# Conv norm of a hybrid encoder layer: means from split sums as fp32r products, and reciprocals issued block by block

## The chip, the cores and the metric

The kernel runs on one core of a Trainium2 chip. The metric is the device time of one execution in microseconds. A change of about 0.2% (2.9 us here) is what a measurement can tell from no change. The core's engines run side by side, each through its own instructions in its own order: TensorE (PE in the profile; its weight loads are PEld), VectorE (DVE), ScalarE (ACT), GpSimd (POOL) and SyncE (SP), which here issues most transfers.

## The reference

One layer of a streaming encoder: one input projection feeds a convolution branch, an attention branch and two gates. The means and variances of the convolution branch are what is changed.

```python
def _layer_norm(x, g, b):
    xf = x.astype(jnp.float32)
    mu = jnp.mean(xf, axis=-1, keepdims=True)
    var = jnp.mean(jnp.square(xf - mu), axis=-1, keepdims=True)
    y = (xf - mu) * lax.rsqrt(var + LN_EPS) * g.astype(jnp.float32) + b.astype(jnp.float32)
    return y.astype(x.dtype)

def _conv_branch(u_ext, w_dw, b_dw, ln_g, ln_b, w_out):
    y = lax.conv_general_dilated(...)            # depthwise, width 31, over 512 channels
    y = jax.nn.silu(_layer_norm(y + b_dw, ln_g, ln_b))
    return jnp.einsum('btc,cd->btd', y, w_out)

# in the layer
u, q, k, v, logf, g_conv, g_attn = _in_proj(x, w_in, b_f)
y_conv = _conv_branch(...)
o_attn = _fox_prompt(q, k, v, logf)             # softmax attention with forget gates
mix = (g_conv * y_conv + g_attn * (o_attn @ w_attn_out)) @ w_o
x1 = layer_norm(ALPHA * x + mix); x2 = layer_norm(ALPHA * x1 + relu(x1 @ w_up)**2 @ w_down)
```

There are 1056 rows (1024 of a new stream, 32 of a running one), 1024 model channels, 512 conv channels, 8 heads of 64.

## The kernel before

**Precision.** Channels lie on the 128 partitions, rows along the free axis. A product of full precision is made of three fp32r products of high and low parts: `hi` is a copy in fp32r (made by ScalarE), `lo` is the value less `hi` (made by VectorE). The weights (`whi`, `wlo`, from `raw`) are split in this way in pieces of 512 columns, ahead of their use.

**Stages.** In the first one (pool `conv`, pool `a`) TensorE makes the projections for the convolution, for v, q and k, and then the first 6 of 16 gate tiles (`gates`). A gate tile is 3 chunks of 352 rows; a chunk is 24 products of 128x352 into one PSUM bank (`ps_g`), which ScalarE copies to `gt` and SyncE writes to memory (`g_s`). In the second stage (pools `b` and `pb`) come attention and, as filling between its products, gates 6 to 15. There the chunks have two PSUM banks (`bbank`: `tag="acc", bufs=2`) and two staging tiles (`GB = 2`).

**The conv branch beside it.** VectorE makes the depthwise convolution and the norm as a generator (`conv`) that is asked for its next piece while TensorE is given projections. The norm works on three blocks of 362 columns (`CC`), each of four tiles `ca`. For each block: the sum of four tiles (`lns_m`), a product with a matrix of 1/512 on TensorE that spreads the mean over all partitions (`ps_mu_c`), subtraction from the four tiles (VectorE), squares (`sq_c`, ScalarE), their sum (`lns_v`), a second such product (`ps_var_c`), a square root (`rstd_c`, ScalarE, which needs a table load before and after it) and its reciprocal (VectorE, in place). Then twelve pieces (block, tile): scale by `rstd_c`, a sigmoid on ScalarE (`csig`), a multiplication, a split into `csh` (ScalarE) and `csl` (VectorE), and four or two writes (`s_s`).

**What sets the order.** The program keeps times of its own for every engine while it writes the instructions (class `Issue`). A generator goes on when what it waits for is due by those times, for a mean 3000 ns after its sum (`MARGIN`). The order in which the instructions are written is the order in which TensorE, VectorE, ScalarE and GpSimd run them; SyncE's is set by a scheduler. When the first stage has no gate left, `I.flush()` writes all that remains of the conv branch, and only then is the second stage written, starting with a table load for the exponential (`tiny`).

Of the kernel before, what the change touches and what calls it, by code (L numbers as in the profile page):

```python
# [9 lines left out]
F32 = mybir.dt.float32  # L10
F32R = mybir.dt.float32r
BF16 = mybir.dt.bfloat16
AF = mybir.ActivationFunctionType
# [4 lines left out]
P = 128  # L18
# [8 lines left out]
C_CONV = 512  # L27
# [12 lines left out]
CC = NC // 3  # L40
# [14 lines left out]
MARGIN = 3000.0  # L55
# [25 lines left out]
class Issue:  # L81
# [116 lines left out]
    def dma(self, out, in_, queue=None):  # L198
        self.run("dma", max(450, Issue.size(out) * out.shape[0] * 4 / 360), [out], [in_])
        out, in_ = (t.bitcast(F32) if t.dtype == F32R else t for t in (out, in_))  # L200
        (queue or self.nc.sync).dma_start(out, in_)

    def mm(self, ps, w, x, start, stop):
        n = self.size(ps)
        self.run("pe", 122 if n == CB else max(107, n / 2.36) if x.dtype != F32 else max(430, n * 1.71), [ps], [w, x])
        self.nc.tensor.matmul(ps, lhsT=w, rhs=x, start=start, stop=stop)  # L206
# [5 lines left out]
    def act(self, out, in_, func, bias=None, **kw):  # L212
        aps = [] if bias is None else [bias]
        self.run("act", self.size(in_) * 0.81 + (62 if self.psum(in_) else 103) + 93 * len(aps),
                 [out] + [v for k, v in kw.items() if k == "accum_out"], [in_] + aps)
        if bias is not None:
            kw["bias"] = bias
        self.nc.scalar.activation(out, in_, func, **kw)  # L218
# [5 lines left out]
    def tt(self, out, a, b, op, eng="dve"):  # L224
        n = self.size(out)
        self.run(eng, n * 1.01 + 80 if eng == "dve" else n * 1.97 + 150, [out], [a, b])
        (self.nc.vector if eng == "dve" else self.nc.gpsimd).tensor_tensor(out, a, b, op)  # L227

    def ts(self, out, a, s1, s2, *ops):
        self.run("dve", self.size(out) * (1.01 if self.psum(a) else 0.51) + 130, [out], [a])  # L230
        self.nc.vector.tensor_scalar(out, a, s1, s2, *ops)

    def stt(self, out, a, s, b, op0, op1):
        self.run("dve", self.size(out) * 1.01 + 140, [out], [a, b])
        self.nc.vector.scalar_tensor_tensor(out, a, s, b, op0, op1)  # L235
# [27 lines left out]
def f32(t):  # L263
    return t.bitcast(F32)
# [3 lines left out]
def hybrid_layer(ctx: ExitStack, tc, io):  # L268
    nc = tc.nc
    I = Issue(nc)  # L270
    dma, mm, act, cp, tt, ts, stt = I.dma, I.mm, I.act, I.cp, I.tt, I.ts, I.stt
    ADD, SUB, MUL, MAX, MIN = ALU.add, ALU.subtract, ALU.mult, ALU.max, ALU.min
# [31 lines left out]
    def par(name, j):  # L304
        return prm[:, PRM[name] + j:PRM[name] + j + 1]
# [186 lines left out]
    with pool("conv") as pv_, pool("a") as pa, pool("pa", space=PSUM) as psa:  # L492
        num = [0]

        def bank(name):
            num[0] += 1
            return psa.tile([P, 512], F32, tag="acc", bufs=8, name=f"ps_{name}_{num[0]}")
# [55 lines left out]
        need_x(4)  # L553
        ones = pa.tile([P, P], F32, name="ones")
        nc.gpsimd.memset(ones, 1.0)
        mean_c = pv_.tile([P, P], F32, name="mean_c")
        nc.gpsimd.memset(mean_c, 1.0 / C_CONV)
        mean_d = const.tile([P, P], F32, name="mean_d")
        nc.gpsimd.memset(mean_d, 1.0 / D)
        zt = pa.tile([P, 9, H], F32, name="zt")  # L560
# [52 lines left out]
        def conv():  # L613
            for j in range(NJ):
                w = [par("w_dw", j * WID + t) for t in range(WID)]
                yield [u[j]]
                ts(ca[j], u[j][:, 0:NC], w[0], par("b_dw", j), MUL, ADD)
                for t in range(1, WID):
                    yield ("dve", 1500)
                    stt(ca[j], u[j][:, t:t + NC], w[t], ca[j], MUL, ADD)  # L620

            blocks = [slice(c * CC, (c + 1) * CC) for c in range(3)]
            tiles = [[ca[j][:, cs] for j in range(NJ)] for cs in blocks]

            def summed(kind, c, src):
                a = pv_.tile([P, CC], F32, tag="lns", bufs=3, name=f"lns_{kind}{c}")
                tt(a, src[0], src[1], ADD)
                for t in src[2:]:
                    tt(a, a, t, ADD)
                return a  # L630

            sums, rstds = [], []
            for c in range(3):
                sums.append(summed("m", c, tiles[c]))
                yield ("dve", 1500)
            for c in range(3):
                yield (MARGIN, [sums[c]])
                mu = bank(f"mu_c{c}")[:, :CC]
                mm(mu, mean_c, sums[c], True, True)
                sq = []  # L640
                for i, t in enumerate(tiles[c]):
                    tt(t, t, mu, SUB)
                    sq.append(pv_.tile([P, CC], F32, tag="lnsq", bufs=4, name=f"sq{i}_c{c}"))
                    act(sq[-1], t, AF.Square)
                sums[c] = summed("v", c, sq)
            for c in range(3):
                yield (MARGIN, [sums[c]])
                var = bank(f"var_c{c}")[:, :CC]
                mm(var, mean_c, sums[c], True, True)
                rstds.append(pv_.tile([P, CC], F32, tag="lnrstd", bufs=3, name=f"rstd_c{c}"))  # L650
                act(rstds[-1], var, AF.Sqrt, bias=eps)
            for r in rstds:
                yield ("dve", 1500)
                I.recip(r, r)
            pieces = [(c, j) for c in range(3) for j in range(NJ)]
            late = last = None
            for piece in pieces + [None, None]:
                yield ("dve", 1500)
                if piece:
                    c, j = piece  # L660
                    y = tiles[c][j]
                    stt(y, y, par("lcg", j), rstds[c], MUL, MUL)
                    sg = pv_.tile([P, CC], F32, tag="csig", bufs=2, name=f"csig{c}_{j}")
                    act(sg, y, AF.Sigmoid, bias=par("lcb", j))
                before, last = last, None
                if late:
                    c, j, z, s = late
                    stt(z, z, par("lcb", j), s, ADD, MUL)
                    hi, lo = (pv_.tile([P, CC], F32R, tag=x, bufs=4, name=f"{x}{c}_{j}") for x in ("csh", "csl"))
                    act(hi, z, AF.Copy)  # L670
                    last = c, j, z, hi, lo
                if before:
                    c, j, z, hi, lo = before
                    tt(lo, z, f32(hi), SUB)
                    for dst, src in ((s_s[0][j], hi), (s_s[1][j], lo)):
                        if c < 2:
                            dma(dst[:, blocks[c]], src)
                        else:
                            e = SEQ - 2 * CC
                            dma(dst[:, 2 * CC:SEQ], src[:, :e])  # L680
                            dma(dst[:, SEQ:T], src[:, CC - DEC:])
                late = (*piece, y, sg) if piece else None
# [47 lines left out]
        for c in range(NCH):  # L730
# [3 lines left out]
            for kind in "ba":  # L734
                glu(kind, 0, c)
                if c == NCH - 1:
                    W.drop()
        I.add(conv(), "conv")
        for j in range(1, NJ):
            for kind in "ba":  # L740
# [11 lines left out]
        for half in range(2):  # L752
            ws = [W.take() for g in range(2)]
            for t in range(9):
# [6 lines left out]
                r = P if t < 8 else DEC  # L761
# [33 lines left out]
        for m in range(4):  # L795
            for name in "qk":
                w = W.take()
                for c in range(NCH):
                    ps = bank(name)[:, :CH]
                    dense(ps, on_x(w, c))  # L800
                    a = pa.tile([P, CH], F32, tag="qk32", bufs=2, name=f"{name}32_{m}_{c}")
# [380 lines left out]
    def cbank(name, tag="acc", bufs=5):  # L1182
        num[0] += 1
        return bank_pool[0].tile([P, 512], F32, tag=tag, bufs=bufs, name=f"ps_{name}_{num[0]}")
# [17 lines left out]
    def tmp(tag, bufs, name):  # L1202
        return ln_pool[0].tile([P, LNW], F32, tag=tag, bufs=bufs, name=name)
# [65 lines left out]
    with pool("ps1", space=PSUM) as bank_pool[0]:  # L1269
# [60 lines left out]
        with pool("l1") as ln_pool[0]:  # L1330
# [60 lines left out]
            for group in GROUPS:  # L1391
                sums = {}
# [51 lines left out]
            sums = combine()  # L1444
            for n, (f, b) in enumerate(order):
# [11 lines left out]
                r = tmp("rp", 5, f"r{f}_{b}")  # L1457
# [343 lines left out]
    for i, cs in enumerate(tail):  # L1801
# [15 lines left out]
        for m in range(KD):  # L1817
            ps = more(m)
            a = acc[m][:, cs]
# [10 lines left out]
    n, tag = cs.stop - cs.start, "n2_last"  # L1830
    tiles = [a[:, cs] for a in acc]
    nth, sq, var, s, held_ps = len(turned), [], None, None, {}
# [24 lines left out]
    mu = cbank("mu_last", "mu", 2)[:, :n]  # L1857
# [122 lines left out]
```

## Time and profile before

| | |
|---|---|
| median of 3 runs | 1444.24 us (1443.33 to 1444.28) |
| the profiled execution | 1444.01 us, its span 1441.4 us, 2.6 us around it |
| TensorE busy | 1425.4 us, 99% of the span |
| VectorE busy | 1119.5 us, 78% |
| ScalarE busy | 683.0 us, 47% |
| granted TensorE clock | 0.998 of full speed |

The stage with the conv norm lies between 263 and 316 us of the span, and the second stage's first gate chunks follow it. A wait of TensorE adds to the time almost one for one; idle time of the others costs nothing by itself.

### The profile page before, as it was taken

What the parts mean: (1) busy time and instruction counts of PE and PEld (TensorE: products, weight loads), DVE (VectorE), ACT (ScalarE), POOL (GpSimd) and SP (SyncE); (2) the same over time, 40 slices, a digit from 0 to 9 for tenths busy, and PEclk for the clock granted to TensorE, in tenths of its full rate; (3) what the DMA queues carried; (4) which work ended last, traced back from release to release, by engine and by line L of the source; (5) the groups of instructions that cost most, each with busy time, mean ns of one, the idle gap of its engine ahead of it and who ended that gap; (6) DMA issues with size and microseconds to landing.
All of it is one profiled execution on the core that took longest, in us unless ns stands there. A gap on an engine that the chain in (4) does not pass through costs nothing.

```text
span 1441.4 us, 27988 instructions
## 1 busy us (share of the span) xinstructions
PE 1425.4 (99%) x10623; PEld 1404.0 (97%) x10623; DVE 1119.5 (78%) x1929; ACT 683.0 (47%) x1446; POOL 124.2 (9%) x183
## 2 busy tenths in 40 slices
PE   9999999999999999999999999999999999999996
PEld 8999999999999999999999999999999999999996
DVE  6998899865666655855797888888976789889668
ACT  5123433465665656543345666676657323321134
POOL 0000000023455533000000000000000000000000
PEclk9999999999999999999999999999999999999999
DMA  7125554287455557425343348766689999884212
GB/s 249 46 61 161 171 172 157 88 273 209 111 152 157 154 153 264 144 83 177 94 135 124 130 151 296 251 239 231 225 287 344 335 317 333 276 321 176 67 45 77
DMA packets 157441, 267.91 MB, mean 186 GB/s; under 512 B 22680, under 2 KB 81272, under 8 KB 157308
## 3 DMA queue, kind: packets, MB, share of 16 engines
q1 hardware_dynamic: 156348, 263.98, 55.4%
q0 software_dynamic: 544, 1.59, 0.5%
q8 instruction: 84, 1.38, 0.4%
q10 hardware_dynamic: 416, 0.56, 0.1%
q14 instruction: 49, 0.40, 0.1%
HBM read 168.29 MB, written 97.74 MB: 185 GB/s over the span
## 4 chain that ended last, share of the span: by engine, by line
PE 97%; DVE 1%; DMA 1%; ACT 0%; issue 0%; SPq 0%; DVEq 0%
PE ps_u L206 18%; PE ps_d L206 17%; PE ps_g L206 13%; PE ps_dn L206 6%; PE ps_o L206 6%; PE ps_up L206 5%; PE ps_v L206 3%; PE ps_yc L206 3%; PE ps_k L206 3%; PE ps_glua L206 3%; PE ps_q L206 3%; PE ps_glub L206 3%; PE ps_yo L206 3%; PE ps_s L206 3%; PE ps_pv L206 2%; PE ps_tr L210 2%
## 5 line engine op out<-in xcount | busy, mean ns | idle before, releaser
L235 DVE SCALAR_TENSOR_TENSOR ca<-u,prm,ca 128x1086 f32<-128x1086 f32 x120 | 161.7, 1347 | 2.4
L206 PE MATMUL ps_g<-xh,whi 128*128 128x352 f32 x384 | 131.7, 343 | 0.0
L218 ACT ACTIVATE swhi<-s 128x512 fp32r<-128x512 f32 x100 | 61.9, 624 | 146.9 <-DVE s L227 134.0
L206 PE MATMUL ps_g<-xh,wlo 128*128 128x352 f32 x384 | 123.7, 322 | 0.0
L206 PE MATMUL ps_g<-xl,whi 128*128 128x352 f32 x384 | 121.5, 322 | 0.0
L206 PE MATMUL ps_u<-tl,swhi 128*128 128x264 f32 x416 | 118.4, 285 | 0.0
L206 PE MATMUL ps_u<-th,swhi 128*128 128x264 f32 x416 | 118.2, 284 | 0.0
L206 PE MATMUL ps_u<-th,swlo 128*128 128x264 f32 x416 | 118.2, 284 | 0.0
L218 ACT ACTIVATE whi<-raw 128x512 fp32r<-128x512 f32 (+1 forms) x120 | 69.6, 624 | 69.6 <-PE ps_glua L206 29.7
L227 DVE TENSOR_TENSOR tl<-ps_tr,th 128x512 fp32r<-128x512 f32 (+2 forms) x96 | 51.4, 552 | 60.2 <-ACT th L218 59.5
L206 PE MATMUL ps_d<-hu_h,swhi 128*128 128x264 f32 x480 | 93.0, 285 | 0.1
L206 PE MATMUL ps_d<-hu_l,swhi 128*128 128x264 f32 x480 | 92.9, 285 | 0.0
L218 ACT ACTIVATE r<-r 128x528 f32<-128x528 f32 (+1 forms) x120 | 73.9, 616 | 37.8 <-DVE r L227 35.5
L227 DVE TENSOR_TENSOR wlo<-raw,whi 128x512 fp32r<-128x512 f32 (+1 forms) x100 | 64.8, 686 | 29.1 <-ACT whi L218 28.9
L227 DVE TENSOR_TENSOR r<-r,ps_u 128x528 f32<-128x528 f32 x91 | 62.6, 699 | 29.6 <-PE ps_u L206 29.6
L206 PEld LDWEIGHTS ps_u<-th,swhi 128*128 128x128 f32 x416 | 78.3, 188 | 0.0
L206 PEld LDWEIGHTS ps_u<-th,swlo 128*128 128x128 f32 x416 | 78.3, 188 | 0.0
L206 PEld LDWEIGHTS ps_u<-tl,swhi 128*128 128x128 f32 x416 | 78.2, 188 | 0.0
L227 POOL TENSOR_TENSOR acc<-acc,lnrest 128x288 f32<-128x288 f32 x4 | 3.0, 787 | 857.6 <-ACT lnrest L218 857.6
L206 PEld LDWEIGHTS ps_d<-hu_h,swhi 128*128 128x128 f32 x480 | 74.6, 189 | 0.3 <-issue 0.2
L206 PEld LDWEIGHTS ps_d<-hu_l,swhi 128*128 128x128 f32 x480 | 74.6, 189 | 0.0
L206 PEld LDWEIGHTS ps_g<-xh,whi 128*128 128x128 f32 x384 | 72.7, 189 | 0.7
(434 smaller groups left out, 4997.8 us busy)
## 6 DMA issues: line engine op xcount, KB each, us to landing
h_s<-sp SPq DMA_DIRECT2D x84, 528.0 KB
raw<-in_w_in_dram SPq DMA_DIRECT2D x63, 256.0 KB
hu_h<-h_s SPq DMA_DIRECT2D x30, 528.0 KB
hu_l<-h_s SPq DMA_DIRECT2D x30, 528.0 KB
sraw<-in_w_up_dram SPq DMA_DIRECT2D x52, 256.0 KB
hu<-h_s SPq DMA_DIRECT2D x24, 528.0 KB
sraw<-in_w_ds_dram SPq DMA_DIRECT2D x48, 256.0 KB
g_s<-gt SPq DMA_DIRECT2D x48, 176.0 KB
```

Of the source, the lines that this page charges most:

```text
L206: self.nc.tensor.matmul(ps, lhsT=w, rhs=x, start=start, stop=stop)
L210: self.nc.tensor.transpose(ps, x, ident)
L218: self.nc.scalar.activation(out, in_, func, **kw)
L227: (self.nc.vector if eng == "dve" else self.nc.gpsimd).tensor_tensor(out, a, b, op)
L235: self.nc.vector.scalar_tensor_tensor(out, a, s, b, op0, op1)
```

## The change

The sum of each block (for the mean and for the variance) is now split: ScalarE makes a high part `csh` in fp32r, VectorE a low part `csl`. The mean is two fp32r products, high and low, into the same bank, in place of one F32 product; the matrix of 1/512 becomes fp32r. The low part of a block is written behind the sum of the next one; the reciprocal of a block behind the square root of the next one. A pause of the generator is gone in front of two reciprocals. Both parts use the tags of the tiles that hold `csh` and `csl` of the result (four buffers each).

```diff
--- before.py
+++ after.py
@@ -553,8 +553,8 @@
         need_x(4)
         ones = pa.tile([P, P], F32, name="ones")
         nc.gpsimd.memset(ones, 1.0)
-        mean_c = pv_.tile([P, P], F32, name="mean_c")
-        nc.gpsimd.memset(mean_c, 1.0 / C_CONV)
+        mean_c = pv_.tile([P, P], F32R, name="mean_c")
+        nc.gpsimd.memset(f32(mean_c), 1.0 / C_CONV)
         mean_d = const.tile([P, P], F32, name="mean_d")
         nc.gpsimd.memset(mean_d, 1.0 / D)
         zt = pa.tile([P, 9, H], F32, name="zt")
@@ -627,31 +627,47 @@
                 tt(a, src[0], src[1], ADD)
                 for t in src[2:]:
                     tt(a, a, t, ADD)
-                return a
+
+                parts = [pv_.tile([P, CC], F32R, tag=x, bufs=4, name=f"{x}_{kind}{c}") for x in ("csh", "csl")]
+                act(parts[0], a, AF.Copy)
+                return a, parts
+
+            def low(a, parts):
+                tt(parts[1], a, f32(parts[0]), SUB)
+                return parts
 
             sums, rstds = [], []
             for c in range(3):
                 sums.append(summed("m", c, tiles[c]))
+                if c:
+                    sums[c - 1] = low(*sums[c - 1])
                 yield ("dve", 1500)
+            sums[2] = low(*sums[2])
             for c in range(3):
-                yield (MARGIN, [sums[c]])
+                yield (MARGIN, sums[c])
                 mu = bank(f"mu_c{c}")[:, :CC]
-                mm(mu, mean_c, sums[c], True, True)
+                for i, a in enumerate(sums[c]):
+                    mm(mu, mean_c, a, i == 0, i == 1)
                 sq = []
                 for i, t in enumerate(tiles[c]):
                     tt(t, t, mu, SUB)
                     sq.append(pv_.tile([P, CC], F32, tag="lnsq", bufs=4, name=f"sq{i}_c{c}"))
                     act(sq[-1], t, AF.Square)
                 sums[c] = summed("v", c, sq)
+                if c:
+                    sums[c - 1] = low(*sums[c - 1])
+            sums[2] = low(*sums[2])
             for c in range(3):
-                yield (MARGIN, [sums[c]])
+                yield (MARGIN, sums[c])
                 var = bank(f"var_c{c}")[:, :CC]
-                mm(var, mean_c, sums[c], True, True)
+                for i, a in enumerate(sums[c]):
+                    mm(var, mean_c, a, i == 0, i == 1)
                 rstds.append(pv_.tile([P, CC], F32, tag="lnrstd", bufs=3, name=f"rstd_c{c}"))
                 act(rstds[-1], var, AF.Sqrt, bias=eps)
-            for r in rstds:
-                yield ("dve", 1500)
-                I.recip(r, r)
+                if c:
+                    I.recip(rstds[c - 1], rstds[c - 1])
+            yield ("dve", 1500)
+            I.recip(rstds[2], rstds[2])
             pieces = [(c, j) for c in range(3) for j in range(NJ)]
             late = last = None
             for piece in pieces + [None, None]:
```

The order moves on all engines between the first sum and the start of attention. **TensorE.** Ahead of the first mean there now stand 30 more gate products than before; behind it 12 to the second mean; behind the third, 78 to the first variance, then 24 to the second. The rows show the second and the third mean. Of before (`lns_m` are the sums, `xh`, `xl` the input, `whi`, `wlo` weights):

```order
L206 MATMUL ps_g_1_78_3009<-xh_145,wlo_2642 128x352
L206 MATMUL ps_mu_c_80_3055<-lns_m_2986,mean_c 128x362
L206 MATMUL ps_g_2_81_3073<-xh_138,whi_2641 128x352
L206 MATMUL ps_g_2_81_3073<-xl_146,whi_2641 128x352
L206 MATMUL ps_g_2_81_3073<-xh_138,wlo_2642 128x352
L206 MATMUL ps_g_2_81_3073<-xh_139,whi_2641 128x352
L206 MATMUL ps_g_2_81_3073<-xl_147,whi_2641 128x352
L206 MATMUL ps_g_2_81_3073<-xh_139,wlo_2642 128x352
L206 MATMUL ps_mu_c_82_3080<-lns_m_2996,mean_c 128x362
L206 MATMUL ps_g_2_81_3073<-xh_140,whi_2641 128x352
```

and of the change:

```order
L206 MATMUL ps_g_2_79_3049<-xh_145,wlo_2642 128x352
L206 MATMUL ps_mu_c_81_3109<-csh_m_2999,mean_c 128x362
L206 MATMUL ps_mu_c_81_3109<-csl_m_3000,mean_c 128x362
L206 MATMUL ps_mu_c_82_3132<-csh_m_3023,mean_c 128x362
L206 MATMUL ps_mu_c_82_3132<-csl_m_3024,mean_c 128x362
L206 MATMUL ps_g_0_83_3156<-xh_138,whi_2759 128x352
L206 MATMUL ps_g_0_83_3156<-xl_146,whi_2759 128x352
```

Two products with 6 gate products between them have become four in a row, and the numbers at the end of `ps_g` tell that a chunk (79) that stood behind the second mean now lies ahead of it.

**VectorE, from the last sum of squares to the first scaled tile** (block 2; `wlo` is the low part of a weight whose high part ScalarE makes). Of before:

```order
L227 TENSOR_TENSOR lns_v_3094<-sq_c_3083,sq_c_3086 128x362
L227 TENSOR_TENSOR lns_v_3094<-lns_v_3094,sq_c_3089 128x362
L227 TENSOR_TENSOR lns_v_3094<-lns_v_3094,sq_c_3092 128x362
L227 TENSOR_TENSOR wlo_3120<-raw_2864,whi_3119 128x512
L227 TENSOR_TENSOR wlo_3120<-raw_2868,whi_3119 128x512
L239 RECIPROCAL rstd_c_3131<-rstd_c_3131 128x362
L239 RECIPROCAL rstd_c_3154<-rstd_c_3154 128x362
L239 RECIPROCAL rstd_c_3180<-rstd_c_3180 128x362
L235 SCALAR_TENSOR_TENSOR ca_258<-ca_258,prm,rstd_c_3131 128x362
```

and of the change:

```order
L227 TENSOR_TENSOR lns_v_3147<-sq_c_3136,sq_c_3139 128x362
L227 TENSOR_TENSOR lns_v_3147<-lns_v_3147,sq_c_3142 128x362
L227 TENSOR_TENSOR lns_v_3147<-lns_v_3147,sq_c_3145 128x362
L227 TENSOR_TENSOR csl_v_3129<-lns_v_3124,csh_v_3128 128x362
L227 TENSOR_TENSOR csl_v_3152<-lns_v_3147,csh_v_3151 128x362
L227 TENSOR_TENSOR wlo_3241<-raw_2970,whi_3240 128x512
L227 TENSOR_TENSOR wlo_3241<-raw_2974,whi_3240 128x512
L239 RECIPROCAL rstd_c_3260<-rstd_c_3260 128x362
L239 RECIPROCAL rstd_c_3293<-rstd_c_3293 128x362
L239 RECIPROCAL rstd_c_3299<-rstd_c_3299 128x362
L235 SCALAR_TENSOR_TENSOR ca_258<-ca_258,prm,rstd_c_3260 128x362
```

Two low parts (`csl_v`) stand behind the sum; the three reciprocals follow each other as before. Further up, a pair of `wlo` that stood at this place is now between the first block's sum of squares and the second block's subtraction, behind ScalarE's `csh_v`, one `gt` and the two `whi`. The pair shown here waits for ScalarE's `csh_v` of block 2, three `gt` (chunks 83 to 85, the last ending 6 gate products ahead of the first variance) and two `whi`; the table load and the first square root stand behind them.

**ScalarE, at the seam of the two stages** (`csig` are sigmoids, `gt_0<-ps_g_0_` without a second number the copy of the second stage's first chunk). Of before:

```order
L218 ACTIVATE csig_2_3458<-ca_260,prm 128x362
L218 ACTIVATE csh_1_3461<-ca_259 128x362
L218 ACTIVATE csig_3_3482<-ca_261,prm 128x362
L218 ACTIVATE csh_2_3485<-ca_260 128x362
L218 ACTIVATE gt_1_3499<-ps_g_1_93_3450 128x352
L218 ACTIVATE csh_3_3510<-ca_261 128x362
L218 ACTIVATE gt_2_3541<-ps_g_2_94_3502 128x352
L218 ACTIVATE whi_3544<-raw_3252 128x512
L218 ACTIVATE whi_3544<-raw_3256 128x512
L218 ACT_TABLE_LOAD
L218 ACTIVATE tiny<-eps 128x1
L218 ACTIVATE gt_0_3622<-ps_g_0_3597 128x352
```

and of the change:

```order
L218 ACTIVATE csig_0_3527<-ca_258,prm 128x362
L218 ACTIVATE csh_3_3530<-ca_261 128x362
L218 ACTIVATE csig_1_3537<-ca_259,prm 128x362
L218 ACTIVATE csh_0_3540<-ca_258 128x362
L218 ACTIVATE csig_2_3547<-ca_260,prm 128x362
L218 ACTIVATE csh_1_3550<-ca_259 128x362
L218 ACTIVATE csig_3_3559<-ca_261,prm 128x362
L218 ACTIVATE csh_2_3562<-ca_260 128x362
L218 ACTIVATE csh_3_3571<-ca_261 128x362
L218 ACT_TABLE_LOAD
L218 ACTIVATE tiny<-eps 128x1
L218 ACTIVATE gt_0_3652<-ps_g_0_3627 128x352
```

The copies of the first stage's last two chunks (93, 94) and the weight pair, which ended the list, now stand ahead of these rows, and nine instructions of the conv branch stand between them and the table load. The second stage's first copy comes behind the conv branch's last `csh` in both. **TensorE again:** in both programs the third chunk of the second stage waits for ScalarE's copy of the first one, whose bank it takes. **SyncE:** in both programs the writes of the second stage's first chunks stand behind all `s_s` writes of the conv branch.

## Rows read from the trace of the kernel before

**Rows 1.** the profile page: the span, the busy time of each engine, and the chain of work that ended last, by engine:

```profile
span 1441.4 us, 27988 instructions
...
PE 1425.4 (99%) x10623; PEld 1404.0 (97%) x10623; DVE 1119.5 (78%) x1929; ACT 683.0 (47%) x1446; POOL 124.2 (9%) x183
...
PE 97%; DVE 1%; DMA 1%; ACT 0%; issue 0%; SPq 0%; DVEq 0%
```

**Rows 2.** the chain of waits, asked of TensorE alone over the whole span: line, what it waited for, microseconds in total, times, the longest:

```profile
PE ps_warm L542 <- DVE warm L537: 1.2, 1, 1.2
PE ps_glub L206 <- ACT xh L218: 1.1, 2, 0.7
PE ps_s L206 <- ACT p L218: 0.6, 1, 0.6
```

**Rows 3.** instructions of TensorE in order of time around the first two means (start, duration, what). A matmul is shown as it passes through, so rows overlap; the step from one start to the next is what it costs the engine. A product in F32 stands as two records merged into one row:

```profile
270.44 0.32 PE L206 MATMUL ps_g<-xh,wlo 128*128 128x352 f32 x1
270.60 0.77 PE L206 MATMUL ps_mu_c<-lns_m,mean_c 128*128 128x362 f32 x2
...
271.37 0.32 PE L206 MATMUL ps_g<-xl,whi 128*128 128x352 f32 x1
...
273.92 0.32 PE L206 MATMUL ps_g<-xh,wlo 128*128 128x352 f32 x1
274.08 0.77 PE L206 MATMUL ps_mu_c<-lns_m,mean_c 128*128 128x362 f32 x2
...
274.85 0.32 PE L206 MATMUL ps_g<-xl,whi 128*128 128x352 f32 x1
```

**Rows 4.** instructions of VectorE in order of time, from the third sum of the conv norm to its reciprocals:

```profile
269.90 0.53 DVE L227 TENSOR_TENSOR lns_m<-ca,ca 128x362 f32<-128x362 f32 x1
...
271.49 1.85 DVE L227 TENSOR_TENSOR ca<-ca,ps_mu_c 128x362 f32<-128x362 f32 x4
...
274.98 1.85 DVE L227 TENSOR_TENSOR ca<-ca,ps_mu_c 128x362 f32<-128x362 f32 x4
...
281.97 1.29 DVE L227 TENSOR_TENSOR wlo<-raw,whi 128x512 fp32r<-128x512 f32 x2
284.23 6.96 DVE L239 RECIPROCAL rstd_c<-rstd_c 128x362 f32<-128x362 f32 x3 [0.97 <-ACT rstd_c L218]
```

**Rows 5.** the same view of VectorE, from the first scaled tile of the conv norm to its last scaled piece:

```profile
291.11 1.00 DVE L235 SCALAR_TENSOR_TENSOR ca<-ca,prm,rstd_c 128x362 f32<-128x362 f32 x2
...
295.37 1.29 DVE L227 TENSOR_TENSOR wlo<-raw,whi 128x512 fp32r<-128x512 f32 x2 [1.04 <-ACT whi L218]
296.58 0.59 DVE L235 SCALAR_TENSOR_TENSOR ca<-ca,prm,rstd_c 128x362 f32<-128x362 f32 x1
...
297.59 0.53 DVE L227 TENSOR_TENSOR csl<-ca,csh 128x362 fp32r<-128x362 f32 x1
298.04 0.59 DVE L235 SCALAR_TENSOR_TENSOR ca<-ca,prm,rstd_c 128x362 f32<-128x362 f32 x1
...
306.46 1.29 DVE L227 TENSOR_TENSOR wlo<-raw,whi 128x512 fp32r<-128x512 f32 x2 [1.04 <-ACT whi L218]
...
312.05 0.59 DVE L235 SCALAR_TENSOR_TENSOR ca<-ca,prm,csig 128x362 f32<-128x362 f32 x1
```

**Rows 6.** instructions of ScalarE in order of time: parts of the stretch in which it serves the gates, the conv norm and the weights:

```profile
283.63 1.01 ACT L218 ACTIVATE rstd_c<-ps_var_c,eps 128x362 f32<-128x362 f32 x2
...
293.98 0.49 ACT L218 ACTIVATE csh<-ca 128x362 fp32r<-128x362 f32 x1
294.37 0.44 ACT L218 ACTIVATE gt<-ps_g 128x352 f32<-128x352 f32 x1
294.72 1.14 ACT L218 ACTIVATE whi<-raw 128x512 fp32r<-128x512 f32 x2
...
312.67 0.51 ACT L218 ACTIVATE csh<-ca 128x362 fp32r<-128x362 f32 x1
...
317.25 1.28 ACT L218 ACT_TABLE_LOAD   x1
318.54 0.20 ACT L218 ACTIVATE tiny<-eps 128x1 f32<-128x1 f32 x1
319.54 0.46 ACT L218 ACTIVATE gt<-ps_g 128x352 f32<-128x352 f32 x1 [0.79 <-PE ps_g L206]
```

**Rows 7.** instructions of TensorE in order of time where the second chunk of gate 6 ends and the third begins (the third begins with the row at 323.15):

```profile
322.99 0.32 PE L206 MATMUL ps_g<-xh,wlo 128*128 128x352 f32 x1
323.15 0.32 PE L206 MATMUL ps_g<-xh,whi 128*128 128x352 f32 x1
```

**Rows 8.** busy time of each engine in short stretches after TensorE's last product: the stretch, its length, then busy microseconds (and count) of PE, PEld, DVE, ACT and POOL, the granted TensorE clock, the busy share of the DMA engines, and GB/s:

```profile
1430.00:1431.00 1.00, 0.08 (x1) 0.00 (x0) 1.00 (x4) 0.00 (x0) 1.00 (x2) 1.00 0.00 0
...
1433.00:1434.00 1.00, 0.00 (x0) 0.00 (x0) 0.97 (x2) 0.00 (x0) 0.04 (x1) 1.00 0.00 0
1434.00:1435.00 1.00, 0.00 (x0) 0.00 (x0) 1.00 (x4) 0.81 (x2) 0.00 (x0) 0.71 0.00 0
```

**Rows 9.** instructions of TensorE in order of time at the start of the program:

```profile
1.19 3.72 PE L542 MATMUL ps_warm<-warm 128*128 128x256 bf16 x19 [1.19 <-DVE warm L537]
```

**Rows 10.** the DMA queue of SyncE in order of time, where the last parts of the conv branch and the first gates of the attention stage are written:

```profile
317.27 0.88 SPq L201 DMA_DIRECT2D s_s<-csl  x2
...
320.18 0.38 SPq L201 DMA_DIRECT2D g_s<-gt  x1
```

## Prediction

> **What bounds the kernel now.** The page comes first: TensorE is busy for 99% of the span, and 97% of the chain that ended last is its own [rows 1]. Next, what TensorE waits for: its longest waits are about 1 us each, at the start of the program, and the longest afterwards is 0.6 us [rows 2]. So the time is TensorE's list of products, nearly without a gap. A shorter list shows in the time one for one, and so does any new wait on TensorE. VectorE and ScalarE have idle time, but both hand things to TensorE: sums for the means, and copies that free PSUM banks. The two questions are therefore how much shorter the list gets, and whether a hand-over is now late.
>
> **The shorter list.** From the gate product ahead of the first mean to the second one behind it, 270.44 to 271.37, are 0.93 us [rows 3]. Between two plain gate products the step is 0.159 us (271.37 to 273.92, 16 steps), so two of them are 0.32 and the F32 mean costs 0.61. The second mean gives the same (273.92 to 274.85). The trace has no fp32r product of 362 columns. The nearest rows are those of 352, in the same format and with weights of the same size: 0.159 x 362/352 = 0.164 us, and two make 0.33. Their bounds are 0.159 (no cost for the ten columns) and 0.30 for half an F32 mean (no gain at all), and I take the first kind, which hundreds of neighbours show. Gain: 6 x (0.61 - 0.33) = 1.7 us. The extra weight load lies beside products, as those of all neighbours do.
>
> **What the new parts cost.** Six copies on ScalarE and six subtractions on VectorE come in. A `csl` takes 0.45 us of VectorE, from start to start (297.59 to 298.04), a `csh` 0.39 of ScalarE (293.98 to 294.37) [rows 5, 6]: 2.7 and 2.3 us that TensorE doesn't see by themselves. The means don't wait for them either. The three sums of a mean end near 273, with their parts, and the first mean now stands 30 gate products further back, at 270.60 + 30 x 0.159 = 275.4. That place, however, is what makes the conv branch late.
>
> **How late the conv branch becomes.** I follow VectorE.
> - In the trace the subtraction begins 0.29 us after the mean's product is through (274.08 + 0.61, then 274.98) [rows 3, 4]. With the product of 0.33 at 275.4 the first subtraction begins at 276.0; before it was 271.49, right behind the sums. That is 4.5 us later.
> - A block of four subtractions and a sum of squares takes 3.49 us (271.49 to 274.98) [rows 4], to 279.5. Then the list now has a pair of `wlo`. It waits for ScalarE's `csh_v` (0.39, after the sum), a `gt` (0.35, 294.37 to 294.72) and the start of a `whi`, which leads its `wlo` by 0.65 (294.72, 295.37); the pair takes 1.21 (295.37 to 296.58) [rows 5, 6]. So the second block begins at 282.2.
> - Two more blocks of 3.49 with one `csl` between: 289.65, against 281.97 [rows 4]: 7.7 later.
> - ScalarE then makes `csh_v` of this block, three `gt` that stand behind it (1.05) and two `whi` (1.14), and loads the table (1.29) [rows 6]: 293.65. The square root leads the first reciprocal by 0.60 (283.63, 284.23), so the reciprocals begin at 294.25, 10.0 later. The variance's product doesn't hold them: 12, then 78 gate products behind the first mean, and the other two means, put it at 290.7. Writing each reciprocal behind the next square root changes nothing, since VectorE runs the same three in a row for 6.9 us: to 301.1.
> - From the first scaling to the last multiplication were 20.94 us (291.11 to 312.05), with two waits of 1.04 for weights [rows 5]. The first pair of weights now comes a piece earlier and is waited for some 0.4 longer; the second wait stays. That gives 322.5. The last `csh` starts 0.62 later and takes 0.51 (312.67) [rows 6]: 323.6.
>
> **Who waits for that.** Behind the last `csh` ScalarE's list has the table load (1.29), `tiny` (0.20) and the copy of the second stage's first chunk (0.46) [rows 6]. The copy ends at 325.55. Before, it began at 319.54 and had waited for TensorE; the conv branch was done 6 us ahead of it. The third chunk takes the bank that this copy frees. It began at 323.15 [rows 7], and with the shorter list TensorE is there at 321.45. So TensorE stands still for **4.1 us**. Nothing else is on its list to do meanwhile; later waits are too small to take the loss back [rows 2].
>
> The bounds of this wait: if ScalarE's work between the sum and the square root were free, the reciprocals would begin 0.9 us after the variance's product is through (0.29 + 0.60), near 291.9, 2.3 us earlier; without the waits for weights (2.5 us) on top, the copy would end before 321.45, and there is no wait. At the upper end, five hand-overs between ScalarE and VectorE each cost a quarter of a microsecond more (0.29 is what one costs): 5.4 us. I take 4.1, because each of its terms is a row.
>
> **The clock.** After its last product, at 1430.08, TensorE was idle; the granted clock still stood at 1.00 in 1433 to 1434 and was 0.71 on average in the microsecond after [rows 8], on its way from 2.4 to 1.2 GHz. A wait of 4.1 us ends just short of that, so I put the clock at nothing in the sum. The Trainium skill ("TensorE: Matmul & The Clock Gate", Part 1) says that an idle stretch sends the clock to its lower level and that sustained work brings it back. By this rule taken alone, the stall would cost more than itself, and the estimate would be 1448.1, the second rival below; the trace agrees that the clock falls after idleness, but shows it once only.
>
> **The sum.** 1444.01 - 1.7 + 4.1 = 1446.4 for a profiled execution. The median of before is 0.23 above its profiled one, so the forecast is 1446.6, 0.17% slower. A measurement tells 0.2% (2.9 us) from no change, so this lies just inside "the same".
>
> **Rivals.**
> - *No wait, 1442.5.* The copy of the first chunk ends before 321.45, and only the 1.7 us are left. For it: VectorE and ScalarE are idle for part of the stretch, and my list of hand-overs may double some. Against it: the place of the mean on TensorE's list alone makes 4.5 us of the delay, and the conv branch had 6 us to spare at the seam; it decides from a delay of about 6 us on, and I count 10.4. Chance 0.15.
> - *The wait and a lower clock, 1448.1.* If the clock falls during the wait, the products behind it run slowly until it is back. At the start of the program 19 products of 256 columns take 3.72 us, 0.196 each [rows 9]; at full speed they would be 256/352 x 0.159 = 0.116. The difference, 1.5 us, is the price. For it: 4.1 us of idleness are close to where the clock fell at the end. Chance 0.16. This one ends slower by more than 0.2%.
> - *A second wait behind SyncE, 1447.9.* The first two chunks of the second stage are written behind all writes of the conv branch. Four writes for a last piece take 1.8 us of SyncE (two take 0.88) [rows 10], more than VectorE's 1.46 for a piece (296.58 to 298.04) [rows 5], so the queue ends near 327.5, and the write of the first chunk, issued at 320.18 before, comes at about 328. The third chunk's copy needs its staging tile. TensorE needs that copy at 333.3, four us after the third chunk ends; it decides if the write lands more than 5 us after its issue, and costs 1.3 us if it takes 6. Chance 0.07.
> - *The forecast: a wait of 3 to 5.4 us*, 1445.4 to 1447.9. Chance 0.60.
>
> **How the numbers follow.** Slower by over 0.2% is above 1447.1: both later rivals (0.23) and the upper third of the forecast's own range (0.18): 0.41. Faster by over 0.2% is below 1441.4, past the whole gain of the shorter list: 0.04 for what I haven't seen. The rest, 0.55, is the same. The range takes in the no-wait case at its lower end and the lower clock at its upper: 1442.4 to 1448.8; the likeliest case's own range is 1445.4 to 1447.9.
>
> **What would show it.** Each mean is two rows with steps of 0.16; the first subtraction begins near 276.0, the reciprocals near 294, the last `csh` near 323; the table load follows at once. TensorE shows one wait of about 4 us for ScalarE's `gt`, near 321, where there is none now, and none on means and variances. The granted clock stays at 1.00 there. The prediction is wrong if that wait is missing (the conv branch is quicker than I count), or if TensorE waits for a `csl`.

## The result, and the profile after

The changed kernel takes 1449.09 us (median of 6 runs, 1448.52 to 1449.71), the kernel before 1444.12 in the runs beside it: a ratio of 1.0034, 95% interval 1.0022 to 1.0045. It is slower by 5.0 us, where 2.4 was forecast, and lies 0.3 us above the range. The profiled execution took 1448.74.

The page of the changed kernel, span, busy times and chain, as in [rows 1]:

```profile
span 1446.5 us, 28009 instructions
PE 1426.0 (99%) x10623; PEld 1405.3 (97%) x10623; DVE 1123.8 (78%) x1935; ACT 685.6 (47%) x1452; POOL 124.3 (9%) x183
PE 94%; DVE 3%; ACT 1%; DMA 1%; issue 1%; SPq 0%; DVEq 0%; ACTq 0%
```

TensorE is busy for about as long as before, although its list is shorter. Its share of the chain falls from 97% to 94%, and VectorE's rises from 1% to 3%. Next TensorE's waits over the whole span, as in [rows 2], and its instructions in order of time at the first mean, the first chunk of the second stage (315.40), the third (327.04) and the products behind it:

```profile
PE ps_g L206 <- ACT gt L218: 5.3, 2, 3.7
```

```profile
275.15 0.33 PE L206 MATMUL ps_mu_c<-csh_m,mean_c 128*128 128x362 f32 x1
275.31 0.33 PE L206 MATMUL ps_mu_c<-csl_m,mean_c 128*128 128x362 f32 x1
275.48 0.33 PE L206 MATMUL ps_g<-xh,whi 128*128 128x352 f32 x1
...
315.40 0.43 PE L206 MATMUL ps_g<-xh,whi 128*128 128x352 f32 x1 [1.63 <-ACT gt L218]
...
327.04 0.43 PE L206 MATMUL ps_g<-xh,whi 128*128 128x352 f32 x1 [3.65 <-ACT gt L218]
...
328.58 0.48 PE L206 MATMUL ps_g<-xh,whi 128*128 128x352 f32 x1
...
331.80 0.42 PE L206 MATMUL ps_g<-xh,wlo 128*128 128x352 f32 x1
...
336.38 0.38 PE L206 MATMUL ps_g<-xh,whi 128*128 128x352 f32 x1
```

A mean costs two steps of 0.16 (275.15 to 275.48), as forecast: 6 x (0.61 - 0.33) = 1.7 us less. But there are two waits, not one, and from 328.58 to 331.80 eleven products take 0.293 each instead of 0.16: 1.5 us. In the spans: -1.7 + 5.3 + 1.5 = +5.1, and they differ by 1446.5 - 1441.4 = 5.1. The last row, the start of the fifth chunk, is needed below. The windows (length, busy time of PE, PEld, DVE, ACT, POOL, granted clock, DMA share, GB/s) show the clock at half, 1.2 GHz:

```profile
326.00:327.00 1.00, 0.00 (x0) 0.00 (x0) 0.00 (x0) 0.99 (x4) 0.94 (x3) 1.00 0.65 190
327.00:328.00 1.00, 0.96 (x6) 0.96 (x7) 0.00 (x0) 0.34 (x1) 0.43 (x2) 1.00 0.58 173
329.00:330.00 1.00, 1.00 (x5) 1.00 (x4) 0.00 (x0) 0.00 (x0) 0.00 (x0) 0.50 0.58 171
332.00:334.00 2.00, 2.00 (x14) 2.00 (x14) 0.00 (x0) 0.00 (x0) 0.00 (x0) 1.00 0.98 375
```

ScalarE at the seam, as in [rows 6], and VectorE's last rows, as in [rows 5]:

```profile
313.44 0.51 ACT L218 ACTIVATE csh<-ca 128x362 fp32r<-128x362 f32 x1 [0.97 <-DMA s_s<-csh]
314.90 0.45 ACT L218 ACTIVATE gt<-ps_g 128x352 f32<-128x352 f32 x1
324.61 0.51 ACT L218 ACTIVATE csh<-ca 128x362 fp32r<-128x362 f32 x1 [1.45 <-DVE csl L227]
325.13 1.28 ACT L218 ACT_TABLE_LOAD   x1
326.54 0.80 ACT L218 ACTIVATE gt<-ps_g 128x352 f32<-128x352 f32 x2
335.81 0.47 ACT L218 ACTIVATE gt<-ps_g 128x352 f32<-128x352 f32 x1 [8.47 <-DMA g_s<-gt]
```

```profile
275.68 1.86 DVE L227 TENSOR_TENSOR ca<-ca,ps_mu_c 128x362 f32<-128x362 f32 x4 [2.78 <-PE ps_mu_c L206]
280.71 1.29 DVE L227 TENSOR_TENSOR wlo<-raw,whi 128x512 fp32r<-128x512 f32 x2 [1.44 <-ACT whi L218]
281.92 1.85 DVE L227 TENSOR_TENSOR ca<-ca,ps_mu_c 128x362 f32<-128x362 f32 x4
294.05 6.96 DVE L239 RECIPROCAL rstd_c<-rstd_c 128x362 f32<-128x362 f32 x3 [1.10 <-ACT rstd_c L218]
322.95 0.58 DVE L235 SCALAR_TENSOR_TENSOR ca<-ca,prm,csig 128x362 f32<-128x362 f32 x1
324.00 0.54 DVE L227 TENSOR_TENSOR csl<-ca,csh 128x362 fp32r<-128x362 f32 x1 [0.47 <-DMA s_s<-csl]
```

The last multiplication is at 322.95, but the last pieces wait for a buffer whose write is under way (`DMA s_s<-csl`), and the last `csh` starts at 324.61. The table load and the copy of the first chunk follow; the third chunk waits for that copy. The copy at 335.81 is the third chunk's own: it waits for the write of the first one, which SyncE issues behind the conv branch's writes:

```profile
328.39 0.89 SPq L201 DMA_DIRECT2D s_s<-csl  x2
329.88 0.86 SPq L201 DMA_DIRECT2D g_s<-gt  x2
```

The first wait is a matter of banks. The second stage's gates take PSUM banks 4 and 5 in both programs. Bank 4 was last held by chunk 88 before; now, with means and chunks in another order, it is chunk 94, the first stage's last, whose copy (314.90) stands behind three instructions of the conv branch (`csh`, `csig`, `csh`); the first of them waited 0.97 us for a write (313.44).

### The profile page after: what moved, and what is told of

Same layout as the page of the kernel before. It is cut to its first block, busy times and chain, and to the rows that moved or that the text cites. A ratio compares the mean times of both kernels' runs of the same rounds, so it can differ in the third digit from the quotient of the medians.

```text
span 1446.5 us, 28009 instructions
## 1 busy us (share of the span) xinstructions
PE 1426.0 (99%) x10623; PEld 1405.3 (97%) x10623; DVE 1123.8 (78%) x1935; ACT 685.6 (47%) x1452; POOL 124.3 (9%) x183
## 4 chain that ended last, share of the span: by engine, by line
PE 94%; DVE 3%; ACT 1%; DMA 1%; issue 1%; SPq 0%; DVEq 0%; ACTq 0%
PE ps_u L206 18%; PE ps_d L206 17%; PE ps_g L206 10%; PE ps_o L206 6%; PE ps_dn L206 6%; PE ps_up L206 5%; PE ps_v L206 3%; PE ps_yc L206 3%; PE ps_k L206 3%; PE ps_glua L206 3%; PE ps_q L206 3%; PE ps_glub L206 3%; PE ps_yo L206 3%; PE ps_s L206 3%; PE ps_pv L206 2%; PE ps_tr L210 2%
```

## Experiments

Theory: the first mean's place on TensorE's list makes the conv branch late, its end holds the first copy, and the fall of the clock costs 1.5 us. Rivals: the added work itself makes it late; the two waits add up; the clock fell for another reason; the writes hold TensorE. Of each edit the line that matters is shown.

**The place of the products.** The pause in front of the means and of the variances is taken out:

```diff
-                yield (MARGIN, sums[c])
+                yield (0.0, sums[c])
```

> The pause between a sum's parts and its product is 0 instead of 3000 ns by the program's own times; nothing else is edited. The first mean then stands 18 gate products earlier on TensorE's list, and the weight pair between the first block's sum of squares and the second block's subtraction moves behind the third. Theory (the conv branch is late because of where the first mean stands): first subtraction near 272.8 instead of 275.7, and 2.6 us more saved by the moved weight pair, so the last csh starts some 5.5 us earlier, near 319; the second stage's first copy ends near 321.5, TensorE waits 0 to 0.5 us at the third chunk, the granted clock stays 1.00, time 1442.2 to 1442.9. Rival (the branch is late because of the added copies, subtractions and buffers themselves, wherever the mean stands): a wait above 2 us stays, time 1446 or more. Second rival (a product now waits for its low part): a TensorE wait on DVE csl of 0.3 us or more.

Measured: 1444.45 us, ratio to the kernel before 1.0001 (0.9992 to 1.0011). VectorE, ScalarE, SyncE, TensorE and a window of it:

```profile
272.98 1.86 DVE L227 TENSOR_TENSOR ca<-ca,ps_mu_c 128x362 f32<-128x362 f32 x4
276.49 1.85 DVE L227 TENSOR_TENSOR ca<-ca,ps_mu_c 128x362 f32<-128x362 f32 x4
...
318.34 0.51 ACT L218 ACTIVATE csh<-ca 128x362 fp32r<-128x362 f32 x1 [0.40 <-DVE ca L235]
320.27 0.45 ACT L218 ACTIVATE gt<-ps_g 128x352 f32<-128x352 f32 x1
330.93 0.46 ACT L218 ACTIVATE gt<-ps_g 128x352 f32<-128x352 f32 x1 [8.81 <-DMA g_s<-gt]
...
323.67 0.94 SPq L201 DMA_DIRECT2D g_s<-gt  x2
...
331.44 0.47 PE L206 MATMUL ps_g<-xh,whi 128*128 128x352 f32 x1 [2.16 <-ACT gt L218]
...
332.00:333.00 1.00, 1.00 (x5) 1.00 (x5) 0.00 (x0) 0.78 (x2) 0.95 (x1) 0.50 0.49 180
```

The theory held for the branch: the first subtraction comes 2.7 us earlier, the second 5.4 (276.49 for 281.92, since the pair of `wlo` no longer stands between them), the last `csh` 6.3, and TensorE doesn't wait at the third chunk. The added work is the same, so the order is what made the branch late: the place of the means and, with it, of the weight pair. The run doesn't separate these two. No product waited for a low part. The first chunk didn't wait either, since in this order bank 4 was last held by chunk 90. But the time stayed some 2 us above the expectation: a wait nobody had named came out at the *fifth* chunk. It takes the bank of the third one, whose copy needs the staging tile of the first one, whose write was issued at 323.67 and was waited for until 330.93, 7.3 us.

**Do the two waits add up?** The second stage's banks moved, with the order of all engines unchanged:

```diff
+        for i in range(2):
+            bbank(f"skip{i}")
         I.filler.append([gates(range(GA, 16), bbank, pb, "g", GB, load_s), None])
```

> The second stage's two gate banks are moved from PSUM banks 4 and 5 to 0 and 1, whose last users in the first stage were copied earlier; the first chunk then needn't wait for the copy of the first stage's last chunk. Theory (the first wait of 1.6 us is absorbed, since the second one ends at a time that the conv branch sets): no wait at the first chunk, 5.3 us instead of 3.7 at the third, its start again near 327.0, time 1448.9 to 1449.4, unchanged. Rival (the two waits add up): the third chunk starts 1.6 us earlier and the time is 1447.4.

Measured: 1449.64 us (1.0038, 1.0025 to 1.0051). TensorE's waits, the third and the fifth chunk, a window:

```profile
PE ps_g L206 <- ACT gt L218: 5.4, 1, 5.4
```

```profile
326.87 0.66 PE L206 MATMUL ps_g<-xh,whi 128*128 128x352 f32 x1 [5.41 <-ACT gt L218]
336.93 0.32 PE L206 MATMUL ps_g<-xh,whi 128*128 128x352 f32 x1
...
325.00:327.00 2.00, 0.13 (x1) 0.13 (x1) 0.54 (x1) 1.99 (x4) 1.89 (x4) 0.51 0.67 198
```

One wait of 5.4, which ends where the two ended. They don't add up: the first was spent ahead of the second. In one piece the wait let the clock fall earlier, and more products ran at half of it: the fifth chunk starts at 336.93 instead of 336.38. The time is half a microsecond above the changed kernel's, which these five runs (1448.96 to 1451.49) can't tell from no change.

**The clock.** 28 products that keep TensorE at work ahead of the third chunk:

```diff
+            for _ in range(28):
+                nc.tensor.matmul(ps[:, :256], lhsT=ident_b, rhs=bfs[:, :256], start=True, stop=True)
```

> 28 bf16 products of 256 columns (some 0.11 us each, 3.1 us in all) into an unused bank stand ahead of the third chunk of gate 6, so that TensorE works while it would wait; they add nothing to the result. Theory (the idle stretch makes the clock fall, and the fall costs 1.5 us): the third chunk still starts near 327.0, the granted clock stays 1.00 from 327 to 332, time 1447.5. Rival (the clock falls there for another reason, or its fall costs nothing): the clock is 0.5 near 329 again, or it isn't and the time stays at 1449.1.

Measured: 1448.95 us (1.0033, 1.0022 to 1.0045). TensorE, ScalarE's copy of the third chunk, and a window:

```profile
323.44 3.23 PE L958 MATMUL ps_fill<-bfs 128*128 128x256 bf16 x28
326.64 0.43 PE L206 MATMUL ps_g<-xh,whi 128*128 128x352 f32 x1
336.26 0.43 PE L206 MATMUL ps_g<-xh,whi 128*128 128x352 f32 x1 [1.67 <-ACT gt L218]
...
335.74 0.46 ACT L218 ACTIVATE gt<-ps_g 128x352 f32<-128x352 f32 x1 [8.80 <-DMA g_s<-gt]
...
329.00:330.00 1.00, 1.00 (x8) 1.00 (x8) 0.00 (x0) 0.00 (x0) 0.00 (x0) 1.00 0.06 11
```

The clock stayed at 1.00, so the idle stretch was what made it fall; and the time did not move. What was won was handed back at the fifth chunk, which starts at 336.26 here and at 336.38 in the changed kernel, right behind the copy that ended at 336.28. (Here the first chunk's write was issued at 331.14, 1.3 us later than in the changed kernel, but the copy that waits for it began at almost the same time, 335.74 and 335.81.) This suggests that two things stand one behind the other: the late branch with the slow clock, and the landing of the write. Taking one away shows the other. The runs with a buffer of their own, below, test that.

**The waits for buffers.** The last two pieces in the buffers of the squares:

```diff
+                    tags = ("lnsq", "lnsq") if c == 2 and j > 1 else ("csh", "csl")
```

> The high and low parts of the last two pieces of the result take the four buffers of the squares, which are free by then, instead of buffers whose writes to memory are still under way. Theory (the last pieces wait 1.4 us for the s_s writes): the last multiplication is followed by its csh after 0.6 us, the last csh starts near 323.2 instead of 324.6, TensorE's wait at the third chunk is 2.2 us instead of 3.7, time 1447.6 if the clock falls again and 1446.1 if the shorter wait leaves it up. Rival (the writes are not what holds the last csh): time and wait unchanged.

Measured: 1448.49 us (1.0030, 1.0020 to 1.0039; 1446.66 to 1451.63). The last `csh` starts at 323.49 instead of 324.61, so the writes had held it by 1.1 us, and the longest wait is 2.7. The clock fell again. The profiled execution took 1447.44, near the expectation; the runs spread too widely for more.

**A buffer for the third chunk's copy, first attempt.** The tile was taken from the softmax tiles, and the program's own times took note of it.

> The changed kernel, but the third chunk of gate 6 is copied into a buffer of its own (a slot of the softmax tiles, not yet in use) instead of the first chunk's staging tile, so that its copy no longer waits for the write of the first chunk. Theory (in the changed kernel TensorE comes to the fifth chunk, whose bank that copy frees, at the very time the copy ends, so the write costs nothing as long as the clock falls): the third chunk's copy follows its products near 331 instead of 335.8; wait of 1.6 and 3.7 us as before, clock down again, time 1448.8 to 1449.3, unchanged. Rival (the write's landing already sets the time): 1447.5.

> The kernel before with the buffer of its own for the third chunk's copy alone. Theory (there the copy waited only for TensorE): unchanged, 1444.0 to 1444.6. Rival (the staging tile cost time in the kernel before too): 1443.5 or less.

These failed as experiments: 1456.91 and 1448.34 us. So did the same buffer with the 28 products (1452.29, where 1447.5 was expected) and with pause 0 (1450.27, where 1442.2 to 1442.8 was). With other times the program wrote the attention stage in another order; in the control TensorE then waits 3.5 us for `tl` there, 0.4 in the kernel before:

```profile
PE ps_tr L210 <- DVE tl L227: 3.5, 4, 1.6
```

**Second attempt, with every engine's order unchanged.** The tile is allocated past the bookkeeping:

```diff
+                    g = staging.pool.tile([P, SEQ], F32, tag="p", bufs=3, name=f"gt{m}_{c}")[:, :CH]
```

> As own_staging (the third chunk's copy gets a buffer of its own in a slot of the softmax tiles), but the program's own times see no difference, so every engine keeps the changed kernel's order instruction for instruction. Theory: the third chunk's copy starts near 331 to 332 instead of 335.8, TensorE's waits of 1.6 and 3.7 us and the fall of the clock stay, and the fifth chunk, which found its bank just free, starts at the same time: 1448.8 to 1449.4, unchanged. Rival (the landing of the write sets the time already): 1447.6.

> The same with the 28 products that keep TensorE busy. Theory (the fall of the clock is worth 1.5 us, but behind it the first chunk's write stood ready to take the same 1.5 us; with both gone the gain shows): clock 1.00 between 327 and 332, no wait for gt of 1 us or more behind 327, time 1447.5. Rival (the fall costs nothing in itself): 1449.0.

> Pause 0 in front of the conv norm's products and the buffer of its own, in the order of margin0. Theory: no wait for gt above 0.3 us between 300 and 345, clock 1.00 there, and margin0's 2.2 us of waiting and its fall of the clock are gone, so that the shorter list shows: 1442.2 to 1442.8. Rival (the same write then holds the fourth chunk's copy, and TensorE waits for that): a wait of 1 us or more between 330 and 345, time 1443.5 or more.

Measured: 1448.80 (1.0035, 1.0022 to 1.0048), 1447.85 (1.0028, 1.0017 to 1.0039) and 1442.62 us (0.9993, 0.9983 to 1.0002). The third chunk's copy and the fifth chunk in the first of these:

```profile
332.93 0.47 ACT L218 ACTIVATE gt<-ps_g 128x352 f32<-128x352 f32 x1 [5.39 <-PE ps_g L206]
...
336.57 0.32 PE L206 MATMUL ps_g<-xh,whi 128*128 128x352 f32 x1
```

The copy no longer waits for a write (a microsecond later than expected, since the slow products end late), and the fifth chunk starts no earlier than in the changed kernel (336.38): without the write in the way it is as slow as with it. With the clock held up as well, the time is 1.0 us less, but the two intervals overlap. In that run TensorE waited up to 0.8 us for a softmax tile, which had to wait for the borrowed slot, so three runs took a tile that is loaded late:

```diff
+                    g = staging.pool.tile([P, 2, PAST], F32, tag="ckr", bufs=1, name=f"gt{m}_{c}")[:, 0, :CH]
```

> The changed kernel with that buffer and with the 28 products that keep TensorE busy in the wait for the first copy. Theory (with the clock up and no write in the way only the 5.3 us of waiting for the first two copies are left: 1443.9 - 1.7 + 5.3): clock 1.00 throughout, 1447.3 to 1447.7, 1.1 to 1.5 us below own_buffer. Rival (the fall of the clock costs nothing in itself): 1448.8.

> As margin0_own_buffer, with the buffer of its own in the tile of the cached keys, which is not loaded before 339, so that no softmax tile waits for a write. Theory (the six means save 1.7 us once nothing at the seam is late): no wait for gt above 0.3 us behind 300, clock 1.00 until the end, 1442.0 to 1442.5, faster than the kernel before by 1.3 to 2.0 us with an interval that leaves out no change. Rival (the products in fp32r save less than half of what the rows say, and the rest of margin0's loss is elsewhere): 1443 to 1444.

> The kernel before with that buffer alone, every engine's order unchanged. Theory (there the copy waited for TensorE, not for the write): 1443.6 to 1444.4, unchanged. Rival (the buffer itself gains): below 1443.2.

Measured: 1447.30 (1.0022, 1.0013 to 1.0031), **1441.97** (0.9990, 0.9981 to 0.9999) and 1443.90 us (1.0001, 0.9992 to 1.0010). A window of the first at the place where the clock was at half, and TensorE's third and fifth chunk there:

```profile
329.00:330.00 1.00, 1.00 (x8) 1.00 (x7) 0.00 (x0) 0.00 (x0) 0.00 (x0) 1.00 0.37 95
```

```profile
327.26 0.43 PE L206 MATMUL ps_g<-xh,whi 128*128 128x352 f32 x1 [0.62 <-ACT gt L218]
...
335.04 0.32 PE L206 MATMUL ps_g<-xh,whi 128*128 128x352 f32 x1
```

and of the second the longest wait of TensorE over the whole span, which is not one for a `gt`, and a window where the clock was at half with pause 0 alone:

```profile
PE ps_warm L548 <- DVE warm L543: 1.2, 1, 1.2
...
332.00:333.00 1.00, 1.00 (x8) 0.62 (x7) 0.79 (x4) 0.37 (x3) 0.00 (x0) 1.00 1.01 241
```

Three things follow. The fifth chunk starts at 336.26 with the clock held up alone, at 336.57 with the write out of the way alone, and at 335.04 with both: the two limits do stand one behind the other, and with the write away the fall of the clock costs 1.5 us (1448.80 against 1447.30). These two times come from different rounds and from buffers in different places; against the kernel before beside each they lie 5.0 and 3.3 us above it, and no run of one reaches into the range of the other (1448.56 to 1449.68, 1446.84 to 1448.19). What is left, 3.3 us, is about the 5.3 us of lateness less the 1.7 of the shorter list. And with the conv branch in time and the write out of the way, the shorter list shows: 2.0 us, where 1.7 were counted, with an interval that just leaves out no change, and none of it comes from the buffer, as the control shows. This version is the fastest of all.

**Low parts at once.** `tt(parts[1], a, f32(parts[0]), SUB)` behind each sum, not behind the next block's:

> The low part of a sum is written right behind the sum, not behind the next block's; the rest is the changed kernel. The first mean stands 6 gate products earlier and the first variance 42. VectorE then waits for each high part, some 0.65 us in six places. Theory (what counts is when the conv branch ends, and the two effects nearly cancel): first subtraction near 274.7, the reciprocals near 292 to 294, TensorE's wait at the third chunk between 2 and 3.7 us, time 1448 to 1449. Rival (the low parts' place is what makes the branch late): the last csh ends before 321, time below 1445.

Measured: 1451.31 us (1.0048, 1.0033 to 1.0063; four runs, 1448.59 to 1451.93), slower than expected. TensorE:

```profile
316.90 0.66 PE L206 MATMUL ps_g<-xh,whi 128*128 128x352 f32 x1 [2.96 <-ACT gt L218]
317.36 0.50 PE L206 MATMUL ps_g<-xl,whi 128*128 128x352 f32 x1
317.66 0.50 PE L206 MATMUL ps_g<-xh,wlo 128*128 128x352 f32 x1
...
336.29 0.43 PE L206 MATMUL ps_g<-xh,whi 128*128 128x352 f32 x1 [1.79 <-ACT gt L218]
```

The branch ends 1.0 us earlier (last `csh` at 323.62), and it helps nothing. The wait at the first chunk is longer, and the clock is low behind it (steps of 0.30 from 317.36); these take the place of the wait that was expected at the third chunk. The fifth starts at 336.29 again, when the write lands. The clock then falls a second time (0.67 on average from 336 to 340), where nothing hides it. The place of the low parts is not what makes the branch late.

**The reciprocals** needed no run: with that part undone the built program has the same instructions in the same order on every engine.

## Why the prediction was wrong, point by point

- **The shorter list, -1.7: right.** The step of a mean's product is 0.16, and the repaired version shows the gain.
- **How late the branch becomes: right nearly to its end.** First subtraction 275.68 (forecast 276.0), reciprocals 294.05 (294.25), last multiplication 322.95 (322.5). The cause was right too: with the means further forward, and the weight pair that moves with them, the last `csh` came 6.3 us earlier. (Two sums of the working are 0.1 higher than the terms written beside them, 282.2 for 282.1 and 293.65 for 293.5, and the chances of its cases add up to 0.98; no conclusion hangs on these.)
- **"The last `csh` starts 0.62 later": wrong.** It started 1.66 later. The step took over a hand-over that had waited for no write (312.05 to 312.67 [rows 5, 6]); here the pieces' buffers were still being written, which the run with other buffers prices at 1.1 us. I had not asked whether the writes kept up with the pieces. So the wait was mis-sized: 5.3 in all instead of 4.1.
- **One wait: wrong in form, not in the sum.** I did not look which bank the second stage's first chunk takes. The bank was that of the first stage's last chunk, and 1.6 of the 5.3 us were spent there; moved elsewhere, they came back at the third chunk.
- **"I put the clock at nothing": this is the step that failed.** The argument was that the one fall in the trace of before came later than 4.1 us of idleness [rows 8]. The clock was still at 1.00 when work resumed, and fell 1.5 us after that. The price was in the rival, 1.5 us by [rows 9], and that is what it cost (eleven products at 0.293 instead of 0.16). The rule of the Trainium skill ("TensorE: Matmul & The Clock Gate", Part 1) that idleness sends the clock down and work brings it back speaks for that rival; the trace agrees, 0.50 behind a wait of 3.65 us and 1.00 again from 332.
- **The second wait behind SyncE, a rival at 0.07: present, but hidden.** The write was issued at 329.88 (328 forecast), and its landing would have held the fifth chunk had the slow products not done so first, as the run with the 28 products shows (a wait of 1.67). It was put beside the wait as something to be added; it stood behind it as a second limit of nearly the same height.

The likeliest case had the right mechanism for the branch and the wait. The lower clock belonged into the sum with it: 1446.6, 1.2 for the longer wait and 1.5 for the clock give 1449.3; 1449.1 was measured.

## What to carry to other kernels

Moving a small product later on the busiest engine's list can cost more than it saves, if a chain of the other engines hangs on it and something at a stage's border hangs on that chain: follow it to the border, with its buffers, its bank and the queue of its writes. Where a wait is removed and the time stays, look for the next limit at the same place before giving up the cause; here it took two removals to see either. And a wait of several microseconds on TensorE can have a price of its own behind it, even if the clock is still up when work resumes.

## What the runs showed of the hardware

In the changed kernel the granted clock did not fall during the wait of 3.65 us but behind it: work resumed at 327.04, the products slowed down at 328.58, and the level was 0.50 until about 331.8. In the run with other banks it was already 0.51 on average in the last two microseconds of the wait of 5.41 us. A wait of 2.16 us at 329 to 331 was followed by a fall too (with the pause at 0: 0.50 in 332 to 333), and there the products were slow from the start, as behind the wait of 2.96 us with the low parts at once. Behind the waits of 1.63 us at 315.40 in the changed kernel and of 1.67 us at 336.26 with the 28 products it stayed at 1.00. When exactly it falls and returns, these runs don't settle. The 28 products held it up in every case.

A write of 176 KB took 7.3 us from issue to its waiting copy while the DMA engines were busy (0.94 to 1.11 in 327 to 330), so a second staging tile wasn't enough there. In the changed kernel it was 5.9 us (329.88 to 335.81).
